# Attention scores over all 128 rows, and local keys in chunks of eight columns

## The chip, the cores and the metric

The kernel runs on one core of a Trainium2 chip. A core has five engines that run side by side: TensorE (PE, matrix products; its weight loads are listed apart as PEld), VectorE (DVE), ScalarE (ACT), GpSimd (POOL) and SyncE (SP), which here issues nearly all transfers; 16 DMA engines carry them. The metric is device time in microseconds, first to last work of one execution; lower is better.

## What is computed

The reference is one inference step of a two-layer backbone over 256 prompt tokens and 2048 latent tokens (a grid of 32 rows by 64 columns), in 1024 channels. Layer 0 is a convolution branch, layer 1 is attention with 16 heads of 64 channels. The part that the change touches is the attention of the latent tokens: each reads a window of 8 rows and 16 columns around it and all 512 cached context keys, in one softmax.

```
q = q * (HEAD_DIM ** -0.5)
# per row r of the grid; blocks j of 16 query columns, 32 key columns each
s_loc = einsum('bjqhd,brjkhd->bhjqrk', qb, k_blk)
s_loc = where(mask, s_loc + bias, NEG_INF)
s_ctx = einsum('bjqhd,blhd->bhjql', qb, k_ctx)
p = softmax(concatenate([s_loc, s_ctx]))
o = einsum(p_loc, v_blk) + einsum(p_ctx, v_ctx)
```

The bias depends on the distance of query and key in rows and columns. Everything is float32.

## The kernel before

**Precision.** Products run on numbers rounded to TensorE's shorter float32 form; each operand is kept as a rounded high part and the low rest, and products of high with high, high with low and low with high are added up. For the scores the keys of a head stand as 128 rows: 64 channels of one part, 64 of the other. `scores` multiplies them with the high part of the queries, held twice (rows 0 to 63 and 64 to 127), in a 128-row product (L1407), and then the half of the rows with the keys' high part with the low part of the queries, in a 64-row product (L1408).

**Stages.** Until about 1800 us of the span run the convolution layer and the projections of attention; there queries, keys and values are split and stored in scratch memory, and `masked_bias` subtracts the position bias from the window mask for every head (L1059). Then come the heads: two halves of eight heads, and in each half the prompt (two heads at a time) and four groups G of eight query rows. A group needs 11, 15, 15 or 12 rows of keys (`KEY_ROWS`).

**A unit** is one head, one group and one block j of 16 query columns: 128 queries against 512 context keys and 32 columns x R rows of local keys. There are 256 units for the latent tokens. A unit runs through these stages:
- four score products into a bank of accumulators S (`scores`, twice);
- on DVE a minimum over the context scores (L1474) and the sum with mask and bias with its minimum (L1476); scores are kept negated;
- on ACT the exponential with its sum (L1480), on DVE the reciprocal (L1481), on POOL the scaling (L1482);
- on TensorE eight transposes of the probabilities (L1492), on ACT their rounding (L1501), on DVE the rest (L109);
- for a pair of blocks the products with the values (L1517 for the context; L1520 or L1524 for the local keys).

**Order.** `attention` writes the order out by hand: a step of the pipeline issues the transposes of unit i - 2, the reductions of unit i, the values of a pair up to unit i - 3 or else a quarter of an output projection tile (`side_chunk`, L1625 to L1627), and then the scores of unit i + 1. TensorE and DVE keep that order; ACT, POOL and SP are ordered by a scheduler. S and the transposes' banks T are held twice. The loads of a head are issued a head ahead, into two buffers each of keys, bias and queries and three of values.

**Layouts.** Local keys, bias, mask, probabilities and values stand in the order (pair of columns, row, 2): the moving operand of the local products reads runs of two columns (8 bytes), each from another grid row. With pairs, ten columns share a product with the values where 10 R rows fit into 128 (groups 0 and 3, R = 11 and 12: `KEY_COLS` is 10); the others take eight (groups 1 and 2, R = 15). With ten, each block has its own four chunks of values, loaded in eight transfers; with eight, the chunks of a pair of blocks overlap, and five products serve both blocks.

Of the kernel before, what the change touches and what calls it, by code (L numbers as in the profile page):

```python
# [11 lines left out]
F32 = mybir.dt.float32  # L12
F32R = mybir.dt.float32r
# [5 lines left out]
P = 128  # L19
D = 1024  # L20
NK = D // P
NPR = 256
NSA = 2048
# [29 lines left out]
# times of the start: of a weight's load, rounding and rest; of the first products; of the modulation; of the input rows  # L53
# [11 lines left out]
# per group of eight query rows: first key row, number of key rows  # L65
KEY_ROWS = [(0, 11), (4, 15), (12, 15), (20, 12)]
# and the key columns that share a product with the probabilities: ten where their rows fit the array, else eight
KEY_COLS = [10, 8, 8, 10]
# per block of 16 query columns: first key column / 8, kind of column window, first bias column
# [6 lines left out]
class Kern:  # L76
    def __init__(self, ctx, tc, io):
# [13 lines left out]
        self.vs_d = d("vs_d", [GW // 2, NSA // GW, 2, NH, 2, DH])  # L91
# [9 lines left out]
    # ---------------------------------------------------------------- helpers  # L101
# [28 lines left out]
    # -------------------------------------------------------------- constants  # L130
    def constants(self):
# [7 lines left out]
        # vectors over channels, one column per 128 channels  # L139
# [7 lines left out]
    def vectors(self, name, srcs, change=None):  # L147
        """Vectors over channels are loaded; the function returned puts them as columns of 128 channels."""
# [23 lines left out]
    def more_constants(self):  # L172
        """The other vectors, in two steps."""
# [10 lines left out]
    def conv_constants(self):  # L184
        """Depthwise taps, [channel, tap], in two steps."""
# [99 lines left out]
    def modulated_steps(self, xts, layer, g, hi, lo, c0, name, rest, on_act=False, flush=(), wide=False):  # L285
        """Rows of xts (already scaled to unit rms), modulated, transposed and split, into columns c0.. of hi, lo."""
# [49 lines left out]
    def halves(self, src, shape, name):  # L336
        """A piece of a weight, rounded, and what is left of it."""
# [15 lines left out]
    # ------------------------------------------------------------- conv layer  # L353
    def conv_layer(self, part_a, part_b):
        """Input projection and depthwise convolution in two chunks of tokens; the second carries on where the first
        ends. Every operation is put at the time it is due by the tensor engine's rate, and all are issued in that
        order: the sums of the first taps of a channel tile run on Pool after its projection, those of the others on
        DVE after that. part_b are the blocks of the second chunk, made along the way."""
# [13 lines left out]
        for s in range(2 * NK):  # L372
# [93 lines left out]
            # the convolution, in two halves of the columns  # L466
# [48 lines left out]
            # the first half: Pool, then DVE in two sums; the second half: DVE, then Pool  # L515
# [28 lines left out]
        # the modulation and the input blocks of the first chunk  # L544
# [62 lines left out]
        # the norm of the first two tiles  # L607
# [13 lines left out]
        # the rest of the modulation, a part of it after each channel tile of the second chunk  # L621
# [5 lines left out]
        # the input blocks of the second chunk  # L627
# [74 lines left out]
        # variance by token on the partitions, then its root's inverse spread over all partitions  # L702
# [34 lines left out]
    def out_weight(self, w, name, res):  # L737
        """w, split, as four tiles of 16 KB per partition: [hi, lo][half of the rows]; two steps for 128 rows."""
# [12 lines left out]
    def conv_out(self, w, blocks, ready, res=None):  # L751
        """Output projection and residual; with res also the modulated input of the next layer."""
# [183 lines left out]
    def bias_rows(self, h):  # L936
        """Position bias of head h for every query of a tile, from row -4 and column -16 of the tile's first."""
# [4 lines left out]
    def na_values(self, blocks, then):  # L942
        """Values of some tokens, [token, channel]; then() where the weights that follow may be loaded."""
# [33 lines left out]
    def na_rest(self, blocks):  # L977
        """Keys, queries and gates of some tokens, [channel, token]."""
# [40 lines left out]
    def store_values(self, c, src, t0, pm):  # L1019
        """Values of four heads of 128 tokens as (hi, lo); those of the sample in the order (pair of columns, row, 2)."""  # L1020
# [21 lines left out]
    def masked_bias(self):  # L1042
        """Window mask less bias of every head, kind of row group and kind of column block: the scores are kept negated."""
# [5 lines left out]
        for h in range(NH):  # L1049
            raw = work([P, BIAS_LEN], "rows", 2, f"rb{h}")  # L1050
            nc.sync.dma_start(raw, self.bias_rows(h))
            for gk, G in enumerate((0, 1, 3)):
                r0, R = KEY_ROWS[G]
                b0 = r0 - 8 * G + 4
                view = lambda ap: ap[:, : 32 * R].rearrange("p (a r c) -> p a r c", a=16, c=2)
# [26 lines left out]
    def keys(self, ct, src, t0, n, pm, nm):  # L1082
        """Keys of two heads, stored as (hi, lo); those of odd heads as (lo, hi)."""
# [45 lines left out]
    def context_values(self):  # L1129
        """Cached values as (hi, lo)."""  # L1130
# [13 lines left out]
    def gated_weights(self):  # L1144
        """The weights of the last projection times the gate of either group, split."""
# [19 lines left out]
    # ------------------------------------------------------------------ phases  # L1165
# [569 lines left out]
```

## Time and profile before

| what | us |
|---|---|
| runs (three): lowest, median, highest | 3113.0, 3113.68, 3121.12 |
| profiled execution: span, first to last instruction | 3115.0 |
| heads of the latent tokens, 1840 to 3070 of the span | 1230 |

The page gives the profiled execution's time as its span alone; it lies 1.3 us above the median of the runs. In the timeline an instruction's row has its start, its duration, the engine, the line of the kernel, what it writes and reads, and the shape; "64*128" are the rows and columns of the weights on TensorE. Ends of products are modelled, so the time from one start to the next tells more than a duration. A row's bracket has the engine's idle time before it and what ended it.

### The profile page before, as it was taken

To read this page: it belongs to the slowest core of one execution; us is meant where nothing else is said; L and a number is where in the kernel's file an instruction comes from. 1 tells how busy PE (TensorE), PEld (TensorE's weight loads), DVE (VectorE), ACT (ScalarE), POOL (GpSimd) and SP (SyncE) were. 2 spreads that over 40 slices of the span, in tenths; PEclk is the share of its full clock that TensorE was granted. 3 is DMA by queue.
4 is the path that set the end of the run, shared out by engine and by line. 5 is a ranking of instruction groups with operands and counts; after the bars stand their busy time and mean duration, and the time that the engine had idled before them with its cause. 6 is when DMAs were issued, how large, how long until landed. Compare 5 with 4: busy or idle time off the path is not lost. (4 is left out here: it accounts for less than half of the span.)

```text
span 3115.0 us, 45374 instructions
## 1 busy us (share of the span) xinstructions
PE 3005.0 (96%) x15951; PEld 2328.0 (75%) x15951; DVE 1857.6 (60%) x3126; ACT 1427.7 (46%) x2538; POOL 1538.2 (49%) x1775
## 2 busy tenths in 40 slices
PE   6999999998999999999999989999999999999998
PEld 4888877775778989999888856666666666666666
DVE  4789999988865000345652046656566656666665
ACT  4466566775533222422222145555555545555553
POOL 4688877886533433622333133444444444444443
PEclk9999999998999999999999979999999999999999
DMA  6242554564355544689998445755545456555442
GB/s 232 86 136 90 197 188 156 183 198 161 122 169 159 149 127 131 187 242 315 347 328 265 125 149 183 204 144 144 143 136 172 137 176 204 164 145 142 132 136 99
DMA packets 429373, 537.40 MB, mean 173 GB/s; under 512 B 42066, under 2 KB 304042, under 8 KB 429017
## 3 DMA queue, kind: packets, MB, share of 16 engines
q1 hardware_dynamic: 429008, 530.42, 55.0%
q10 hardware_dynamic: 136, 4.07, 0.3%
q8 instruction: 127, 2.08, 0.3%
q14 instruction: 102, 0.83, 0.1%
HBM read 351.34 MB, written 187.13 MB: 173 GB/s over the span
## 5 line engine op out<-in xcount | busy, mean ns | idle before, releaser
L1482 POOL TENSOR_SCALAR sa_p<-sa_p,sa_m 128x992 f32<-128x992 f32 (+2 forms) x256 | 288.2, 1126 | 528.9 <-DVE sa_m L1481 424.9
L1501 ACT CAST sa_pt<-sa_T 128x512 fp32r<-128x512 f32 (+2 forms) x512 | 276.0, 589 | 540.9 <-PE sa_T L1492 540.8
L500 DVE SCALAR_TENSOR_TENSOR cv<-u,dw,cv 128x640 f32<-128x640 f32 (+2 forms) x570 | 427.9, 822 | 3.8 <-ACT cv L496 2.9
L1474 DVE TENSOR_REDUCE sa_m<-sa_S 128x1 f32<-128x512 f32 x256 | 176.9, 691 | 403.3 <-PE sa_S L1408 390.1
L109 DVE TENSOR_TENSOR sa_pt<-sa_T,sa_pt 128x512 fp32r<-128x512 f32 (+2 forms) x512 | 329.2, 684 | 4.1 <-ACT sa_pt L1501 3.8
L349 PE MATMUL ci_ps<-h_s_hi,ci_wh 128*128 128x512 f32 x768 | 307.1, 400 | 2.0 <-DVE shift L237 1.0
L1492 PEld LDWEIGHTS sa_T<-ident,sa_p 128*128 128x128 f32 (+2 forms) x2048 | 221.5, 140 | 115.0 <-issue 57.3
L351 PE MATMUL ci_ps<-h_s_hi,ci_wl 128*128 128x512 f32 x768 | 303.2, 395 | 0.0
L350 PE MATMUL ci_ps<-h_s_lo,ci_wh 128*128 128x512 f32 x768 | 302.9, 394 | 0.0
L1492 PE MATMUL sa_T<-ident,sa_p 128*128 128x128 f32 (+2 forms) x2048 | 284.1, 282 | 0.9 <-DVE sa_pt L109 0.9
L1480 ACT ACTIVATE sa_p<-sa_S,sa_m 128x992 f32<-128x992 f32 (+2 forms) x256 | 269.4, 1052 | 7.6 <-DVE sa_m L1476 4.5
L481 POOL TENSOR_TENSOR cv_s<-cv_s,cv_p 128x519 f32<-128x519 f32 (+1 forms) x155 | 233.3, 1505 | 69.7 <-DVE cv_s L504 49.0
L478 ACT ACTIVATE cv_p<-u,dw 128x640 f32<-128x640 f32 (+2 forms) x326 | 240.9, 770 | 55.0 <-POOL cv_s L481 35.7
L481 POOL TENSOR_TENSOR cv_p<-cv_p,cv_p 128x520 f32<-128x520 f32 (+1 forms) x155 | 227.7, 1469 | 26.8 <-ACT cv_p L478 19.2
L1407 PE MATMUL sa_S<-a_k,a_qh 128*128 128x480 f32 (+2 forms) x256 | 181.3, 708 | 0.0
L1408 PE MATMUL sa_S<-a_k,a_ql 64*128 64x480 f32 (+2 forms) x256 | 180.3, 704 | 0.0
L1517 PE MATMUL sa_O<-sa_pt,cv 128*128 128x256 f32 x1024 | 177.1, 295 | 0.3 <-DVE 3_14_of L1538 0.3
L1476 DVE CUSTOM_DVE_ANT_0 sa_S<-sa_S,a_bm,sa_m 128x480 f32<-128x480 f32 (+2 forms) x256 | 170.9, 668 | 9.0
L349 PEld LDWEIGHTS ci_ps<-h_s_hi,ci_wh 128*128 128x128 f32 x768 | 145.5, 189 | 39.2 <-ACT cv_p L478 2.5
L351 PEld LDWEIGHTS ci_ps<-h_s_hi,ci_wl 128*128 128x128 f32 x768 | 145.1, 189 | 33.6
L350 PEld LDWEIGHTS ci_ps<-h_s_lo,ci_wh 128*128 128x128 f32 x768 | 145.4, 189 | 31.1
L106 POOL TENSOR_TENSOR nis_wl<-nis_w,nis_wh 128x1024 fp32r<-128x1024 f32 x24 | 60.9, 2540 | 183.0 <-ACT nis_wh L341 157.8
(846 smaller groups left out, 7495.5 us busy)
## 6 DMA issues: line engine op xcount, KB each, us to landing
adaw<-in_ada_w SPq DMA_DIRECT2D x24, 1024.0 KB
ci_w<-in_conv_w_in SPq DMA_DIRECT2D x48, 512.0 KB
a_bm<-bm_d SPq DMA_DIRECT2D x32, 720.0 KB
x_s<-in_x_sample SPq DMA_DIRECT2D x32, 512.0 KB
vs_d<-v_s SPq DMA_DIRECT2D x128, 128.0 KB
a_qh<-qh_d SPq DMA_DIRECT2D x64, 256.0 KB
o_x<-x_d SPq DMA_DIRECT2D x32, 512.0 KB
a_v<-vs_d SPq DMA_DIRECT2D x128, 120.0 KB
```

The source lines that it names most:

```text
L109: self.nc.vector.tensor_tensor(out=lo, in0=src, in1=hi.bitcast(F32), op=ALU.subtract)
L349: self.nc.tensor.matmul(out, wh[:, k, :], hh[:, k, :], start=k == 0, stop=False)
L350: self.nc.tensor.matmul(out, wh[:, k, :], hl[:, k, :], start=False, stop=False)
L351: self.nc.tensor.matmul(out, wl[:, k, :], hh[:, k, :], start=False, stop=k == NK - 1)
L478: nc.scalar.activation(t, st["u"][:, c0 + tap : c1 + tap], AF.Copy, scale=self.dw[:, ct, tap : tap + 1])
L481: nc.gpsimd.tensor_tensor(out=st["sum", half], in0=st["sum", half], in1=st[half, tap], op=ALU.add)
L500: nc.vector.scalar_tensor_tensor(out=out, in0=u, scalar=w, in1=first, op0=ALU.mult, op1=ALU.add)
L1407: self.nc.tensor.matmul(out, q, k, start=True, stop=False)
L1480: nc.scalar.activation(p[:, n], S[:, n], AF.Exp, scale=-1.0, bias=m[:, 2:3], accum_out=m[:, 3:4])
L1482: nc.gpsimd.tensor_scalar(out=p[:, n], in0=p[:, n], scalar1=m[:, 3:4], scalar2=1.0, op0=ALU.mult, op1=ALU.mult)
L1492: nc.tensor.transpose(t[:w, c * P : c * P + P], p[:, x + c * w : x + c * w + w], self.ident)
L1501: nc.scalar.copy(pt[:w, 0, part, :, at], t)
```

## The change

It sets one chunk width, `CW = 8`, for all groups. Local keys, bias, mask, probabilities and values stand as (eight columns, row, 8); the low part of the queries is loaded for each head onto all 128 rows, as the high part is; both score products run over all 128 rows, so that low times low is added too; the value rows of a head come in one transfer. The separate treatment of groups 0 and 3 (ten columns, the block at the other end of its bank, the clearing of padding on POOL) is gone. Comments and docstrings are gone too, so line numbers shift by some 10 to 20 (`scores` from L1407 and L1408 to L1397 and L1398).

```
-KEY_COLS = [10, 8, 8, 10]
+CW = 8
-        self.vs_d = d("vs_d", [GW // 2, NSA // GW, 2, NH, 2, DH])
+        self.vs_d = d("vs_d", [GW // CW, NSA // GW, CW, NH, 2, DH])
...
-                view = lambda ap: ap[:, : 32 * R].rearrange("p (a r c) -> p a r c", a=16, c=2)
+                view = lambda ap: ap[:, : 32 * R].rearrange("p (a r c) -> p a r c", a=4, c=CW)
...
-        return bass.AP(ap.tensor, ap.offset, [ap.ap[0], [2, 16], [BIAS_COLS, R], [1, 2]])
+        return bass.AP(ap.tensor, ap.offset, [ap.ap[0], [CW, 4], [BIAS_COLS, R], [1, CW]])
...
-        hd.q = T("qh", [P, n], F32R, nm + "_qh")
-        src = self.qh_d[h * DH : h * DH + DH, a : a + n]
-        nc.sync.dma_start(hd.q.bitcast(F32), bass.AP(src.tensor, src.offset, [[0, 2], *src.ap]))
-        if b == 0:
-            hd.grp["ql"] = T("ql", [P, n], F32R, nm + "_ql")
-            nc.sync.dma_start(hd.grp["ql"].bitcast(F32), self.ql_d[rows, a : a + n])
-        else:
+        hd.q, hd.ql = (T(t, [P, n], F32R, f"{nm}_{t}") for t in ("qh", "ql"))
+        for t, d in ((hd.q, self.qh_d), (hd.ql, self.ql_d)):
+            src = d[h * DH : h * DH + DH, a : a + n]
+            nc.sync.dma_start(t.bitcast(F32), bass.AP(src.tensor, src.offset, [[0, 2], *src.ap]))
+        if b:
...
-        src = self.vs_d[:, r0 : r0 + R, :, hd.h].rearrange("a r c s d -> a (r c) (s d)")
-        if cw == 8:
-            for g in range(4):
-                self.nc.sync.dma_start(v[g * 2 * R : (g + 1) * 2 * R], src[g::4].rearrange("a x e -> x a e"))
-            return
-        for i, first in enumerate((0, 12)):
-            for c in range(4):
-                a = first + 5 * c
-                self.nc.sync.dma_start(v[: 10 * R, 4 * i + c], src[a : a + 5])
+        src = self.vs_d[:, r0 : r0 + R, :, hd.h].rearrange("a r c s d -> (r c) a (s d)")
+        self.nc.sync.dma_start(v[: CW * R], src)
...
-    def scores(self, out, q, ql, k, odd):
-        half = slice(DH, P) if odd else slice(0, DH)
+    def scores(self, out, q, ql, k):
         self.nc.tensor.matmul(out, q, k, start=True, stop=False)
-        self.nc.tensor.matmul(out, ql[half], k[half], start=False, stop=True)
+        self.nc.tensor.matmul(out, ql, k, start=False, stop=True)
...
-        kw = hd.k[:, :, 8 * JFIRST[j] : 8 * JFIRST[j] + 32].rearrange("p r (a c) -> p a r c", c=2)
+        kw = hd.k[:, :, CW * JFIRST[j] : CW * JFIRST[j] + 32].rearrange("p r (a c) -> p a r c", c=CW)
...
-        if wide:
-            x = 512 - 40 * R if jj else 512 + nl
-            nc.gpsimd.memset(p[:, x : x + 8 * R], 0.0)
-            at = 512 - 40 * R if jj else 512
...
-            for c in range(4) if cw == 10 else ():
-                nc.tensor.matmul(o, v[:w, 4 * pair + c].rearrange("p s d -> p (s d)"), loc[:, 256 * c : 256 * c + 256], start=False, stop=s == 1 and c == 3)
-            for c in (0, 4, 1, 2, 3) if cw == 8 else ():
+            for c in (0, 4, 1, 2, 3):
```

On TensorE the order of the steps is the same; what differs are the value products of groups 0 and 3. Here is the end of a step of group 0 before (values of head 0, then the scores of head 1, block 3; `cv` are context values, `a_0_v` the local ones, `ck` context keys, `a_1_k` local ones):

```order
L1517 MATMUL sa_0_O<-sa_0_2_pt,cv_16370 128x256 x4
L1520 MATMUL sa_0_O<-sa_0_2_pt,a_0_v 128x256 x4
L1407 MATMUL sa_1_3_S<-ck_16372,a_1_qh 128x512
L1408 MATMUL sa_1_3_S<-ck_16372,a_0_ql 128x512
L1407 MATMUL sa_1_3_S<-a_1_k,a_1_qh 128x352
L1408 MATMUL sa_1_3_S<-a_1_k,a_0_ql 128x352
```

And the same place on TensorE now:

```order
L1499 MATMUL sa_0_O<-sa_0_2_pt,cv_16372 128x256 x4
L1504 MATMUL sa_0_O<-sa_0_2_pt,a_0_v 128x128 x2
L1504 MATMUL sa_0_O<-sa_0_2_pt,a_0_v 128x256 x3
L1397 MATMUL sa_1_3_S<-ck_16374,a_1_qh 128x512
L1398 MATMUL sa_1_3_S<-ck_16374,a_1_ql 128x512
L1397 MATMUL sa_1_3_S<-a_1_k,a_1_qh 128x352
L1398 MATMUL sa_1_3_S<-a_1_k,a_1_ql 128x352
```

Four local value products of 256 columns have become two of 128 and three of 256, and head 1 reads low queries of its own (`a_1_ql`) instead of those shared with head 0.

On SP, the transfers of a head in group 0 (head 3, and the low queries of head 4) before, where `a_3_v` are value chunks and `a_3_bm` bias and mask:

```order
L1402 DMA a_3_v<-vs_d 110x1x128
L1367 DMA a_3_qh<-qh_d 128x1x512
L1359 DMA a_3_k<-ks_d 128x704
L1402 DMA a_3_v<-vs_d 110x1x128
L1364 DMA a_3_bm<-bm_d 128x3x352
L1402 DMA a_3_v<-vs_d 110x1x128 x6
L1370 DMA a_4_ql<-ql_d 128x512
```

And those of the same head on SP now:

```order
L1393 DMA a_3_v<-vs_d 88x8x128
L1370 DMA a_3_qh<-qh_d 128x1x512
L1361 DMA a_3_k<-ks_d 128x704
L1370 DMA a_3_ql<-ql_d 128x1x512
L1366 DMA a_3_bm<-bm_d 128x3x352
```

Eight transfers of values have become one that stands first, and the low queries of every head come before its bias.

More of the change, by code (lines that the diff above doesn't have):

```diff
@@ L1348, in load_head @@
                 nc.sync.dma_start(hd.q[:, e].bitcast(F32), bass.AP(src.tensor, src.offset, [[0, 2], *src.ap]))
-            hd.ql = T("ql", [P, n], F32R, nm + "_ql")
-            nc.sync.dma_start(hd.ql.bitcast(F32), self.ql_d[rows, a : a + n])
+            hd.ql = T("ql", [P, 2, NPR], F32R, nm + "_ql")
+            for e in range(2):
+                src = self.ql_d[(h + e) * DH : (h + e + 1) * DH, 0:NPR]
+                nc.sync.dma_start(hd.ql[:, e].bitcast(F32), bass.AP(src.tensor, src.offset, [[0, 2], *src.ap]))
             hd.v = T("vl", [P, 2, 4, DH], F32R, nm + "_v")
@@ L1364, in load_head @@
         nc.sync.dma_start(hd.bm[:, :, :nl], self.bm_d[h, GKIND[G]][:, :, :nl])
-        hd.q = T("qh", [P, n], F32R, nm + "_qh")
-        src = self.qh_d[h * DH : h * DH + DH, a : a + n]
-        nc.sync.dma_start(hd.q.bitcast(F32), bass.AP(src.tensor, src.offset, [[0, 2], *src.ap]))
-        if b == 0:
-            hd.grp["ql"] = T("ql", [P, n], F32R, nm + "_ql")
-            nc.sync.dma_start(hd.grp["ql"].bitcast(F32), self.ql_d[rows, a : a + n])
-        else:
+        hd.q, hd.ql = (T(t, [P, n], F32R, f"{nm}_{t}") for t in ("qh", "ql"))
[3 more added lines that the diff above has]
+        if b:
             hd.z = T("z", [P, n], F32, nm + "_z")
             nc.sync.dma_start(hd.z, self.zn_d[rows, a : a + n])
-        hd.ql = hd.grp["ql"]
         self.load_context(hd.ctx, h)
@@ L1418, in prompt_unit @@
                 cs = slice(u * P, u * P + P)
-                self.scores(S[:, (2 * e + u) * NPR : (2 * e + u + 1) * NPR], hd.q[:, e, cs], hd.ql[:, cs], hd.k[:, e], e)
+                self.scores(S[:, (2 * e + u) * NPR : (2 * e + u + 1) * NPR], hd.q[:, e, cs], hd.ql[:, e, cs], hd.k[:, e])
         yield
@@ L1463, in sample_unit @@
         S = self.bank("S", nm + "_S", 2, 1024)
-        cw = KEY_COLS[G]
-        wide, jj = cw == 10, j % 2
-        a, at = (512, 512 - nl) if wide and jj else (0, 512)
-        ctx, loc = S[:, a : a + 512], S[:, at : at + nl]
-        kw = hd.k[:, :, 8 * JFIRST[j] : 8 * JFIRST[j] + 32].rearrange("p r (a c) -> p a r c", c=2)
-        self.scores(ctx, hd.q[:, cs], hd.ql[:, cs], hd.ctx[h][0], b)
-        self.scores(loc, hd.q[:, cs], hd.ql[:, cs], kw, b)
+        jj = j % 2
+        ctx, loc = S[:, :512], S[:, 512 : 512 + nl]
+        kw = hd.k[:, :, CW * JFIRST[j] : CW * JFIRST[j] + 32].rearrange("p r (a c) -> p a r c", c=CW)
+        self.scores(ctx, hd.q[:, cs], hd.ql[:, cs], hd.ctx[h][0])
+        self.scores(loc, hd.q[:, cs], hd.ql[:, cs], kw)
         yield
@@ L1478, in sample_unit @@
         p = T("p", [P, 1024], F32, nm + "_p")
-        n = slice(min(a, at), min(a, at) + 512 + nl)
+        n = slice(0, 512 + nl)
         nc.scalar.activation(p[:, n], S[:, n], AF.Exp, scale=-1.0, bias=m[:, 2:3], accum_out=m[:, 3:4])
@@ L1482, in sample_unit @@
         nc.gpsimd.tensor_scalar(out=p[:, n], in0=p[:, n], scalar1=m[:, 3:4], scalar2=1.0, op0=ALU.mult, op1=ALU.mult)
-        if wide:
-            x = 512 - 40 * R if jj else 512 + nl
-            nc.gpsimd.memset(p[:, x : x + 8 * R], 0.0)
-            at = 512 - 40 * R if jj else 512
         yield
         ts = []
-        for part, w, x in ((0, P, a), (1, cw * R, at)):
+        for part, w, x in ((0, P, 0), (1, CW * R, 512)):
             t = self.bank("T", f"{nm}_T{part}", 2)
@@ L1498, in sample_unit @@
         for part, w, t in ts:
-            at = 1 - jj if part == 0 or wide else jj
+            at = 1 - jj if part == 0 else jj
             nc.scalar.copy(pt[:w, 0, part, :, at], t)
@@ L1511, in sample_values @@
         c0 = JFIRST[2 * pair]
-        cw = KEY_COLS[hd.G]
-        w = cw * KEY_ROWS[hd.G][1]
+        w = CW * KEY_ROWS[hd.G][1]
         for s in range(2):
@@ L1695, in neighbourhood_masks @@
             ok_c = (col >= cs[:, None]) & (col < cs[:, None] + KC)
-            ok = ok_c.reshape(P, 16, 1, 2) & ok_r.reshape(P, 1, R, 1)
+            ok = ok_c.reshape(P, 4, 1, CW) & ok_r.reshape(P, 1, R, 1)
             out[gk, :, jk, : 32 * R] = np.where(ok, 0.0, FAR).reshape(P, -1)
```

1 line of the change is left out of this document (removed).

## The prediction

> **What bounds the kernel now.** I read the page first for the shares, then the busy time of the attention stage by engine, then TensorE's timeline there row by row, because a busy TensorE says nothing of how fast each product goes.
>
> ```profile
> span 3115.0 us, 45374 instructions
> PE 3005.0 (96%) x15951; PEld 2328.0 (75%) x15951; DVE 1857.6 (60%) x3126; ACT 1427.7 (46%) x2538; POOL 1538.2 (49%) x1775
> 1840.00:3070.00 1230.00, 1208.91 (x6026) 805.34 (x6026) 760.70 (x1628) 638.93 (x1211) 545.51 (x881) 0.98 0.53 155
> ```
>
> The last row is the stage of the sample's heads (after the stretch: its length, busy time of PE, weight loads, DVE, ACT, POOL, then granted clock, DMA share, GB/s). TensorE is busy 1208.91 of 1230 us at a clock of 0.98; DVE 62%, ACT 52%, POOL 44%, the DMA engines 0.53. TensorE is the bound, and nobody else is near.
>
> Two steps of the pipeline on TensorE (start, duration, instruction; the next start is what counts, since durations overlap):
>
> ```profile
> 2109.43 1.09 PE L1492 MATMUL sa_T<-ident,sa_p 128*128 128x128 f32 x8
> ...
> 2110.59 0.39 PE L1626 MATMUL o<-w2l,0_1_y2h 128*128 128x512 f32 x1
> 2110.82 0.39 PE L1627 MATMUL o<-w2h,0_1_y2l 128*128 128x512 f32 x1
> ...
> 2111.75 0.40 PE L1407 MATMUL sa_S<-ck,a_qh 128*128 128x512 f32 x1
> 2112.08 0.49 PE L1408 MATMUL sa_S<-ck,a_ql 64*128 64x512 f32 x1
> 2112.50 0.77 PE L1407 MATMUL sa_S<-a_k,a_qh 128*128 128x480 f32 x1
> 2113.20 0.77 PE L1408 MATMUL sa_S<-a_k,a_ql 64*128 64x480 f32 x1
> 2113.90 1.09 PE L1492 MATMUL sa_T<-ident,sa_p 128*128 128x128 f32 x8
> ...
> 2116.36 0.74 PE L1524 MATMUL sa_O<-sa_pt,a_v 120*128 120x128 f32 x5
> 2116.94 0.39 PE L1407 MATMUL sa_S<-ck,a_qh 128*128 128x512 f32 x1
> ...
> 2119.07 1.09 PE L1492 MATMUL sa_T<-ident,sa_p 128*128 128x128 f32 x8
> ```
>
> A step with a piece of the output projection lasts 4.47 us (2109.43 to 2113.90), one with values 5.17 (to 2119.07), without a gap. A 128-row product of 512 contiguous columns is followed by the next start after 0.23 us (2110.59, 2110.82): 0.45 ns a column. The four score products of a unit take 0.33 + 0.42 + 0.70 + 0.70 = 2.15 us, where four products at 0.45 ns a column (512 + 512 + 480 + 480 columns) would take 0.89. That difference is what the change goes for, and it has two sources.
>
> ```profile
> L1408 PE MATMUL sa_S<-ck,a_ql 64*128 64x512 f32 x256 | 128.0, 500 | 0.4 <-DMA a_ql<-ql_d 0.4
> L1407 PE MATMUL sa_S<-ck,a_qh 128*128 128x512 f32 x256 | 103.7, 405 | 5.6 <-DMA a_qh<-qh_d 5.6
> L1407 PE MATMUL sa_S<-a_k,a_qh 128*128 128x480 f32 x128 | 98.4, 769 | 0.0
> L1408 PE MATMUL sa_S<-a_k,a_ql 64*128 64x480 f32 x128 | 97.8, 764 | 0.0
> L1407 PE MATMUL sa_S<-a_k,a_qh 128*128 128x384 f32 x64 | 42.4, 663 | 0.0
> ```
>
> *Rows.* The context products read contiguous keys, yet the pair takes 0.33 + 0.42 = 0.75 instead of 0.46: about 0.10 is lost going from 128 rows to 64 and 0.19 by the 64-row product that has 128 rows before and behind it. *Runs.* The local products with 128 and with 64 rows take the same (769 and 764 ns), so their length is no matter of rows; from 384 to 480 columns they grow by 106 ns, 1.1 ns a column, against 0.45 for contiguous keys. They read runs of two columns. Both local products have a change of rows ahead or behind: 0.70 less 0.19 leaves 0.51 for 480 columns, 1.06 ns each, the same figure from the other side.
>
> **The change part by part.** *All 128 rows in both score products.* The context pair falls from 0.75 to 0.46: 0.29 x 256 units = 74 us. (That loading 64 or 128 rows of weights might differ is excluded by rows that take 0.23 with 128.)
>
> *Runs of eight.* No row shows runs of eight; the ends are contiguous keys (0.45 ns a column) and runs of two (1.06). If each break between runs costs a fixed (1.06 - 0.45) x 2 = 1.2 ns, runs of eight cost 0.45 + 1.2 / 8 = 0.60. If instead a run takes the longer of 2.1 ns (what two columns take) and its own length, eight columns take 3.6 ns and the rate is 0.45. Both readings lie near the contiguous row; I take the middle, 0.52. The other two widths, before:
>
> ```profile
> 1911.53 0.62 PE L1407 MATMUL sa_S<-a_k,a_qh 128*128 128x352 f32 x1
> 1912.09 0.62 PE L1408 MATMUL sa_S<-a_k,a_ql 64*128 64x352 f32 x1
> 1912.64 1.09 PE L1492 MATMUL sa_T<-ident,sa_p 128*128 128x128 f32 x8
> ...
> 2410.44 0.67 PE L1407 MATMUL sa_S<-a_k,a_qh 128*128 128x384 f32 x1
> 2411.03 0.67 PE L1408 MATMUL sa_S<-a_k,a_ql 64*128 64x384 f32 x1
> 2411.63 1.09 PE L1492 MATMUL sa_T<-ident,sa_p 128*128 128x128 f32 x8
> ```
>
> Local pairs now: 1.40 us (480 columns, groups 1 and 2, 128 units), 1.19 (384, group 3, 64 units), 1.11 (352, group 0, 64 units). At 0.52: 0.50, 0.40, 0.37. Gain 0.90 x 128 + 0.79 x 64 + 0.74 x 64 = 213 us; at 0.45 it is 230, at 0.60 it is 193.
>
> The Trainium skill ("Advanced Engine Details and Errata", SBUF Cachelines) has 16-byte lines of which two consecutive hits suffice for full rate. Runs of two 4-byte columns hit a line twice, so by that rule they are not slow at all; 1.06 ns a column says otherwise, and the measurement decides. For runs of eight the rule gives the contiguous end, 230 us instead of 213 and a time lower by 17.
>
> *Values of groups 0 and 3.* Five products instead of four for each half (hi, lo) of a pair of blocks: 32 heads x 2 pairs x 2 halves = 128 times. Five take 0.58 (2116.36 to 2116.94, above), four take 0.48:
>
> ```profile
> 2409.20 0.64 PE L1520 MATMUL sa_O<-sa_pt,a_v 120*128 120x256 f32 x4
> 2409.68 0.40 PE L1407 MATMUL sa_S<-ck,a_qh 128*128 128x512 f32 x1
> ```
>
> 0.10 x 128 = 13 us lost, on the bound itself. The products and transposes then use 88 or 96 rows or columns, no width that the trace shows; the nearest rows, 110 and 120, flow like 128, so I take nothing. The other end is that they stall as 64 rows do: two halves x two changes x 0.19 x 64 pairs = 49 us.
>
> *Steps that TensorE did not bound by much.* What is late next is DVE's chain:
>
> ```profile
> 2109.60 0.69 DVE L1474 TENSOR_REDUCE sa_m<-sa_S 128x1 f32<-128x512 f32 x1 [2.21 <-PE sa_S L1408]
> ...
> 2112.42 0.16 DVE L1481 RECIPROCAL sa_m<-sa_m 128x1 f32<-128x1 f32 x1 [0.16 <-ACT sa_p L1480]
> 2112.61 0.69 DVE L1538 TENSOR_TENSOR 1_4_of<-sa_O,1_5_t 64x512 f32<-64x512 f32 x1
> ```
>
> 3.0 us a step from reduction to reciprocal, and 0.7 more in one step of a head's four: 12.7 a head. TensorE's new steps are 4.47 - 1.19 = 3.28 and 5.17 - 1.19 = 3.98, 14.5 a head, so it stays the bound there. Not in steps with neither values nor output work:
>
> ```profile
> 1867.52 1.10 PE L1492 MATMUL sa_T<-ident,sa_p 128*128 128x128 f32 x8
> ...
> 1870.32 0.88 PE L1492 MATMUL sa_T<-ident,sa_p 128*128 128x128 f32 x6
> ...
> 2959.70 1.09 PE L1492 MATMUL sa_T<-ident,sa_p 128*128 128x128 f32 x8
> ...
> 2962.55 0.66 PE L1492 MATMUL sa_T<-ident,sa_p 128*128 128x128 f32 x4
> ```
>
> These are the first and the last of 14 such steps, 2.8 to 3.1 us, already about DVE's 3.0: they keep their length, and 14 x 1.05 = 15 us of the gain is lost. 18 steps with half of a pair's values, counted in the same timeline, fall about 0.25 below DVE's chain: 5 more.
>
> *Loads.* The low halves of the queries come once a head, not once for two: 128 KB more a head on average, and values as one transfer instead of four or eight, of fewer bytes in groups 0 and 3. SyncE's issues of the eight cost 10.77 us for seven in one place, and near it lies the only long wait of TensorE in this stage:
>
> ```profile
> 1911.27 10.77 SPq L1402 DMA_DIRECT2D a_v<-vs_d  x7
> 1920.73 0.76 PE L1407 MATMUL sa_S<-ck,a_qh 128*128 128x512 f32 x1 [5.60 <-DMA a_qh<-qh_d]
> 2115.00:2117.00 2.00, 2.00 (x19) 2.00 (x18) 1.84 (x5) 1.86 (x4) 1.80 (x5) 1.00 1.02 287
> 2121.00:2123.00 2.00, 2.00 (x7) 0.84 (x5) 1.06 (x3) 1.03 (x2) 0.70 (x2) 1.00 0.12 47
> ```
>
> In groups 1 and 2 the engines run full for a while (1.02 at 287 GB/s) and then idle (0.12), so some 2.8 MB a head (keys 480 KB, bias 720, queries 512, values 480, gates 128, residual rows 512 by their tiles) fit into 14.5 us, but with less room than in 19.3. Bounds: 9 us won (that wait goes, with the slow step behind it) to 25 lost; I take 6 lost, for group 0, where the output weights arrive too.
>
> *Bias, masks, the stored order of the values.* Their work lies in the projections of attention. There DVE is busy 69 of 100 us under a TensorE that is busy 98:
>
> ```profile
> L1059 DVE TENSOR_TENSOR bm<-mask,rb 128x480 f32<-128x480 f32 x48 | 42.3, 934 | 3.3 <-DMA bm_d<-bm 3.3
> 1450.00:1550.00 100.00, 98.44 (x563) 86.76 (x562) 69.24 (x98) 24.62 (x42) 32.13 (x19) 1.00 0.99 341
> ```
>
> Same operations, longer runs: nothing, between a few microseconds either way if the transfers there, at 0.99, shift. POOL's dropped clearing of padding and the prompt's low halves: nothing, beside TensorE's work (the prompt's eight units could win 5).
>
> **Sum.** 74 + 213 - 13 - 20 - 6 = 248 off 3115.0 gives 2867; the median of the runs lies 1.3 below the profiled span, so **2866**.
>
> **Rivals.** *The gather stays slow:* a scattered read costs 1.06 ns a column whatever its runs. Then 74 + 0.19 x 2 x 256 = 171, less 13, 10 (fewer short steps hurt) and 6: 2972. For it: only contiguous and runs of two are in the trace. Against: 32-byte runs have a quarter of the breaks.
>
> *Rows do not matter*, and the 0.33 and 0.42 have another cause that stays: only the gather's gain, 2 x 0.54 ns x (480 x 128 + 384 x 64 + 352 x 64) = 117, less 13, 8 and 6: about 3024. The Trainium skill speaks for it ("TensorE: Matmul & The Clock Gate", "Why this matters for your kernels"): one product with few rows takes as long as one with 128. The rows speak against it: 500 against 405 ns for the same 512 columns, and 0.42 against 0.23 to the next start.
>
> *Narrow products stall* (88 and 96 rows): 49 us more, 2915. *Loads become a wait in most heads:* 64 heads x 1 us gives 2930.
>
> *Slower:* the single value transfer and the doubled low halves land so late that each head waits for its loads. A head takes 19.3 us now (twice 4.47 + 5.17); those 2.8 MB must come in that time, so the kernel gets slower only if the chip brings less than some 145 GB/s here; at 140, 64 heads x 0.7 us gives about 3160. Against it: 287 GB/s above.
>
> **How the numbers follow.** Forecast (2818 to 2910) 0.70; gather stays slow 0.10; rows do not matter 0.03; narrow products stall 0.05; loads wait 0.08; slower 0.03; nothing moves 0.01. The range goes down to 2818 (contiguous rate 17, loads 15 better, prompt 5, and 10 for the 0.01 us to which each of a unit's four starts is read) and up to 2915 (0.60 ns a column 20, loads 19 worse, or the stall of narrow products); it holds the forecast and about half of the two cases next to it. Within 0.3% (what a measurement can tell from no change) is 9 us: only if nothing moves or two rivals meet, 0.02; slower 0.03; faster 0.95.
>
> **What would show it.** Right: L1397 and L1398 on contiguous context keys both at about 405 ns with starts 0.23 apart; local ones of 480 columns with starts 0.22 to 0.29 apart; steps near 3.3 and 4.0 us; short steps unchanged at DVE's 3.0. Wrong: local starts still 0.5 apart, rows of TensorE waiting for a_qh, a_ql or a_v at heads' beginnings, or DVE's reciprocal ending after the next step's first transposes in most steps.

## The result, and the profile after

The changed kernel takes 3238.1 us (median of four runs, 3231.5 to 3242.8); the kernel before took 3114.7 beside it. The ratio is 1.040, 95% interval 1.038 to 1.041: **slower**, by 123 us, where I had forecast 248 us less.

First the page's head of the changed kernel, then the row of its heads by the windows view (columns as in the prediction: stretch, its length, busy time of PE, weight loads, DVE, ACT, POOL, then granted clock, DMA share, GB/s):

```profile
span 3239.6 us, 45214 instructions
...
PE 2801.7 (86%) x16079; PEld 2417.1 (75%) x16079; DVE 1858.0 (57%) x3126; ACT 1440.1 (44%) x2538; POOL 1501.6 (46%) x1647
```

```profile
1840.00:3160.00 1320.00, 999.04 (x6049) 881.84 (x6048) 756.20 (x1609) 645.53 (x1211) 508.49 (x747) 0.86 0.52 150
```

TensorE is busy 203 us less than before (2801.7 against 3005.0): the products did get cheaper. But among the heads it now works 999 of 1320 us instead of 1209 of 1230, at a clock of 0.86 instead of 0.98. No other engine is near its limit, and the DMA share is 0.52, as before. What TensorE waits for, by the view of waits from 1830 us on (what stood, in which line, for what; then total us, times, longest):

```profile
PE sa_S L1398 <- DMA a_ql<-ql_d: 213.8, 52, 7.9
PE sa_S L1397 <- DMA a_qh<-qh_d: 41.0, 16, 7.6
PE pa_S L1398 <- DMA aNone_ql<-ql_d: 34.7, 10, 5.5
...
PE pa_S L1397 <- DMA aNone_k<-ks_d: 8.8, 1, 8.8
...
PE pa_O L1442 <- DMA aNone_v<-vp_d: 5.6, 1, 5.6
```

That is 304 us for loads, 255 of it for the queries of the heads, in 68 places. One of them, on TensorE's timeline of the changed kernel, with a step of the forecast kind ahead of it (start, duration, instruction; in brackets the idle time before it):

```profile
2131.87 0.40 PE L1397 MATMUL sa_S<-ck,a_qh 128*128 128x512 f32 x1
2132.11 0.40 PE L1398 MATMUL sa_S<-ck,a_ql 128*128 128x512 f32 x1
2132.34 0.42 PE L1397 MATMUL sa_S<-a_k,a_qh 128*128 128x480 f32 x1
2132.59 0.42 PE L1398 MATMUL sa_S<-a_k,a_ql 128*128 128x480 f32 x1
2132.84 1.04 PE L1475 MATMUL sa_T<-ident,sa_p 128*128 128x128 f32 x8
...
2135.12 0.46 PE L1397 MATMUL sa_S<-ck,a_qh 128*128 128x512 f32 x1
2142.28 0.79 PE L1398 MATMUL sa_S<-ck,a_ql 128*128 128x512 f32 x1 [6.69 <-DMA a_ql<-ql_d]
...
2143.67 1.91 PE L1475 MATMUL sa_T<-ident,sa_p 128*128 128x128 f32 x8
```

The four score products of a unit start 0.24, 0.23, 0.25 and 0.25 us apart, 0.97 in all where they took 2.15. Then the next head's high part has come, its low part has not, and TensorE stands for 6.7 us. What the DMA engines do meanwhile, by windows of the changed kernel, and the DMA view of 2138 to 2141 us (packets, MB, share of the time of 16 engines):

```profile
2138.00:2140.00 2.00, 0.00 (x0) 0.00 (x0) 0.00 (x0) 0.00 (x0) 2.00 (x5) 0.76 0.13 49
2140.00:2142.00 2.00, 0.00 (x0) 0.00 (x0) 0.00 (x0) 0.00 (x0) 0.22 (x1) 0.50 0.14 52
```

```profile
DMA packets 72, 0.15 MB, mean 49 GB/s; under 512 B 0, under 2 KB 0, under 8 KB 72
...
q1 hardware_dynamic: 72, 0.15, 13.1%
```

This is the row to learn from. TensorE waits for a transfer while the DMA share is 0.13. A share of 13.1% of 16 engines is 2.1 engines: **two engines work without a pause and fourteen do nothing**. In the trace's records of the single transfers, exactly two are under way for 93% of these 3 us and three for the rest. They carry only packets of 2 KB (0.15 MB / 72), the size of a row of the queries' tiles, each in 0.131 x 16 x 3 us / 72 = 87 ns. A load of 256 KB is 128 such packets: over two engines 5.6 us. Before the change a head had one such load (the high part, with the two copies outermost in its source); its low part came as 128 plain rows and once for two heads. Now it has two. The row of 0.12 at 47 GB/s that the prediction quotes from the kernel before (2121 to 2123 us) is two engines' worth as well, and I read it as idleness. By the records its packets are of 5,760 bytes (rows of bias), 512 (values) and 4,096 (output rows), two at a time for most of it: what the two engines still had to carry of other loads, after all others were done.

The rest of the stage's traffic also passes through these two, by its sixteenth. Is that enough to fill them? The DMA view of the changed kernel, 1840 to 3160 us (issues: times, KB each):

```profile
q1 hardware_dynamic: 131865, 196.61, 51.9%
...
a_qh<-qh_d SPq DMA_DIRECT2D x63, 256.0 KB
a_ql<-ql_d SPq DMA_DIRECT2D x63, 256.0 KB
```

In engine-time 0.519 x 16 x 1320 = 10,960 us were worked. The queries' 126 loads are 126 x 128 x 87 ns = 1,400 of it, 700 on each of the two; of the other 9,560 each engine has 598. The two are busy for some 1,300 of 1,320 us, 98%, while the mean says 52%. This is an estimate; it takes all other traffic as spread evenly over the sixteen. The records of the single transfers agree with it: in these 1,320 us exactly two are under way for 36% of the time, some 480 us, and fewer than two for only 3%. In the heads of the kernel before it is 16% with two and 12% with fewer. That is the theory: **A, two DMA engines set the pace of the heads**. SyncE's issues fit a backlog too: one that takes 0.51 us elsewhere stood for 8 us, and the next load, that of the keys, could only be issued at 2140.89:

```profile
2125.75 0.51 SPq L1370 DMA_DIRECT2D a_ql<-ql_d  x1
...
2132.79 8.00 SPq L1370 DMA_DIRECT2D a_qh<-qh_d  x1
```

Against A stood **B**, the single transfer of values ahead of the queries delays them; **C**, the 128 KB more a head are too many bytes; and **D**, the low part stands behind other loads in SyncE's order.

### The profile page after: what moved, and what is told of

Its sections match the earlier page's. It is cut to its first block, busy times and chain, and to the rows that moved or that the text cites. A ratio compares the mean times of both kernels' runs of the same rounds, so it can differ in the third digit from the quotient of the medians.

```text
span 3239.6 us, 45214 instructions
## 1 busy us (share of the span) xinstructions
PE 2801.7 (86%) x16079; PEld 2417.1 (75%) x16079; DVE 1858.0 (57%) x3126; ACT 1440.1 (44%) x2538; POOL 1501.6 (46%) x1647
## 5 line engine op out<-in xcount | busy, mean ns | idle before, releaser
L1469 POOL TENSOR_SCALAR sa_p<-sa_p,sa_m 128x992 f32<-128x992 f32 (+2 forms) x256 | 280.2, 1095 | 744.7 <-DVE sa_m L1468 660.1
L1484 ACT CAST sa_pt<-sa_T 128x512 fp32r<-128x512 f32 (+3 forms) x512 | 278.3, 587 | 573.2 <-PE sa_T L1475 572.7
L109 DVE TENSOR_TENSOR sa_pt<-sa_T,sa_pt 128x512 fp32r<-128x512 f32 (+3 forms) x512 | 331.6, 683 | 7.6 <-ACT sa_pt L1484 3.1
L1475 PE MATMUL sa_T<-ident,sa_p 128*128 128x128 f32 (+3 forms) x2048 | 298.5, 294 | 14.1 <-DVE sa_pt L109 14.1
L1398 PE MATMUL sa_S<-ck,a_ql 128*128 128x512 f32 x256 | 118.0, 461 | 213.8 <-DMA a_ql<-ql_d 213.8
L1475 PEld LDWEIGHTS sa_T<-ident,sa_p 128*128 128x128 f32 (+3 forms) x2048 | 265.0, 148 | 46.1 <-POOL None_y1l L106 13.4
L1398 PEld LDWEIGHTS sa_S<-ck,a_ql 128*128 128x128 f32 x256 | 52.6, 206 | 237.6 <-DMA a_ql<-ql_d 235.0
L1504 PE MATMUL sa_O<-sa_pt,a_v 120*128 120x256 f32 (+5 forms) x1280 | 201.6, 290 | 1.3 <-DMA a_v<-vs_d 1.3
L1499 PE MATMUL sa_O<-sa_pt,cv 128*128 128x256 f32 x1024 | 192.5, 314 | 0.3 <-DVE 3_14_of L1518 0.3
L1504 PEld LDWEIGHTS sa_O<-sa_pt,a_v 120*128 120x128 f32 (+2 forms) x1280 | 179.7, 204 | 1.6 <-DMA a_v<-vs_d 1.6
```

Of the source, the lines that this page charges most:

```text
L109: self.nc.vector.tensor_tensor(out=lo, in0=src, in1=hi.bitcast(F32), op=ALU.subtract)
L1469: nc.gpsimd.tensor_scalar(out=p[:, n], in0=p[:, n], scalar1=m[:, 3:4], scalar2=1.0, op0=ALU.mult, op1=ALU.mult)
L1475: nc.tensor.transpose(t[:w, c * P : c * P + P], p[:, x + c * w : x + c * w + w], self.ident)
L1484: nc.scalar.copy(pt[:w, 0, part, :, at], t)
L1504: nc.tensor.matmul(dst, v[:w, c0 + c].rearrange("p s d -> p (s d)"), loc[:, lo:hi], start=False, stop=s == 1 and c == 3)
```

## The experiments

**The low halves in two loads of 64 rows.** Same bytes, one more issue; each load's outermost dimension is now 64 rows.

```
-        for t, d in ((hd.q, self.qh_d), (hd.ql, self.ql_d)):
-            src = d[h * DH : h * DH + DH, a : a + n]
-            nc.sync.dma_start(t.bitcast(F32), bass.AP(src.tensor, src.offset, [[0, 2], *src.ap]))
+        src = self.qh_d[h * DH : h * DH + DH, a : a + n]
+        nc.sync.dma_start(hd.q.bitcast(F32), bass.AP(src.tensor, src.offset, [[0, 2], *src.ap]))
+        for e in range(2):
+            nc.sync.dma_start(hd.ql[e * DH : e * DH + DH].bitcast(F32), self.ql_d[h * DH : h * DH + DH, a : a + n])
```

> The changed kernel, but the low halves of the queries come in two loads of 64 rows (one for each copy) instead of one load whose outermost dimension is the two copies. Same bytes, one more issue on SyncE per head. Theory A (a load with the two copies outermost is served by two DMA engines only: 128 packets of 2 KB at 84 ns each over two engines are 5.4 us, twice per head, in front of those engines' share of everything else): TensorE's waits for a_ql (213.8 us in the changed kernel's attention) fall below 30 us, the granted clock returns to 0.97 or more, and the time is 2850 to 2900 us. Theory B (the single value transfer delays what stands behind it): no change, 3238 within 20 us. Theory C (the 128 KB more per head are simply too many bytes): no change, 3238 within 20 us.

3031.6 us, 0.973 of before (0.971 to 0.976). Waits of this kernel from 1830 us on, and its heads by windows:

```profile
PE sa_S L1399 <- DMA a_ql<-ql_d: 60.9, 26, 5.5
PE sa_S L1398 <- DMA a_qh<-qh_d: 37.0, 9, 8.0
```

```profile
1840.00:2990.00 1150.00, 984.96 (x6226) 874.57 (x6227) 772.44 (x1655) 664.18 (x1245) 524.27 (x771) 0.92 0.65 176
```

207 us come back without a byte less, so B and C fall: C as a cause of these 207 us, B as the cause of the larger part. Yet it is 130 us short of what A expected, and the waits for a_ql are twice the 30 I allowed. My size was wrong: one load on two engines stays. By the rows above (an estimate, with 63 heads again) the two have 63 x 128 x 87 ns / 2 = 351 us of it and 704 of the rest, 1,055 of 1,150 us: 92%, still little room for loads that come in bursts; by the records exactly two transfers are under way for 21% of this time.

**Both halves in two loads of 64 rows** (the same edit for `qh`).

> As the run before, and the high halves in two loads of 64 rows too. Theory A: the two engines lose the second 5.4 us per head as well; the remaining waits for a_qh (41.0 us in the changed kernel) go down, and the time is 0 to 25 us below that of the run before, 2835 to 2890 us. No stretch in which the mean DMA share stands near 0.13 (two of sixteen) for longer than 2 us. Theories B and C: 3238 within 20 us.

2918.2 us, 0.938 (0.936 to 0.940). Waits of this kernel from 1830 us on:

```profile
PE pa_S L1399 <- DMA aNone_ql<-ql_d: 36.4, 10, 6.0
PE sa_T L1476 <- DVE sa_pt L109: 20.9, 12, 11.6
PE sa_S L1399 <- DMA a_ql<-ql_d: 10.9, 6, 3.3
```

The heads' queries are down from 255 to 11 us. What is left belongs mostly to the prompt, whose queries still have the two copies outermost. The time is 28 us above the range, and stretches with two engines alone, expected to be no longer than 2 us, are left: in 2328 to 2331 us, where the prompt's low halves are loaded, the share is again that of 2.2 engines, now with packets of 1 KB.

```profile
q1 hardware_dynamic: 137, 0.14, 13.5%
```

The gain over the run before is 113 us, not the 0 to 25 expected, for the reason just given.

**Controls.** Values in four loads again, low halves split by columns with the copies still outermost, and low halves issued by ScalarE:

```
+        for g in range(4):
+            self.nc.sync.dma_start(v[g * 2 * R : (g + 1) * 2 * R], src[g * 2 * R : (g + 1) * 2 * R])
```

> The changed kernel, but a head's values come in four loads of a quarter of the rows each (22 to 30 rows) instead of one. Theory A: no help, 3225 to 3270 us, TensorE's waits for a_ql stay above 180 us. Theory B (the single value transfer is the cause): the waits go, 2850 to 2900 us. Theory C: 3238 within 20 us.

```
+        for e in range(2):
+            src = self.ql_d[h * DH : h * DH + DH, a + e * n // 2 : a + (e + 1) * n // 2]
+            nc.sync.dma_start(hd.ql[:, e * n // 2 : (e + 1) * n // 2].bitcast(F32), bass.AP(src.tensor, src.offset, [[0, 2], *src.ap]))
```

> The changed kernel, but the low halves come in two loads that split the 512 columns and keep the two copies outermost in each. Same bytes, same number of loads as in the run that splits by rows, packets of 1 KB instead of 2. Theory A: each load still runs on two engines, 256 packets of 1 KB at 46 ns over two engines are 5.9 us: no help, 3230 to 3300 us. Rival (one load more, or a shorter load, is what helps): 2850 to 2900 us as with rows.

```
+            q = nc.sync if t is hd.q else nc.scalar
+            q.dma_start(t.bitcast(F32), bass.AP(src.tensor, src.offset, [[0, 2], *src.ap]))
```

> The changed kernel, but the low halves of the sample heads' queries are issued by ScalarE instead of SyncE, with the two copies still outermost. Theory A: the same two DMA engines serve both queues, so the change of queue does not help: 3200 to 3300 us. Rival D (the low halves are late because they stand behind other loads on SyncE, in its order of issue): TensorE's waits for a_ql fall under 60 us and the time under 3050 us.

They took 3289.2, 3255.0 and 3236.4 us, one run each. None helps. The first is 19 us above A's range; why four loads are worse than one was not pursued. Waits of TensorE, first with values in four loads (1840 to 3200 us), then with the low halves on ScalarE's queue (1840 to 3160 us):

```profile
PE sa_S L1399 <- DMA a_ql<-ql_d: 213.0, 51, 7.3
```

```profile
PE sa_S L1398 <- DMA a_qh<-qh_d: 190.4, 39, 12.3
```

The first removes B. In the second the wait has only changed its name: the low halves no longer stand in SyncE's line, so now the high halves come last, and the time is the same. D falls; another queue did not bring more engines. The DMA view of this run, 1974 to 1977 us, has packets of both queues side by side (q1 is SyncE's, q10 has the low halves), and together they still fill no more than 2.1 engines:

```profile
q1 hardware_dynamic: 37, 0.07, 6.6%
q10 hardware_dynamic: 36, 0.07, 6.4%
```

The split by columns tells that it isn't the number of loads that helped: two loads by rows brought 207 us, two by columns lost 17.

**The prompt too.** All loads of queries on 64 rows.

> As the run with both halves of the sample heads' queries in two loads of 64 rows (2918 us), and the prompt heads' queries in such loads too (they still had the two copies outermost, packets of 1 KB on two engines). Theory A: the waits that were left, 36.4 us of pa_S for aNone_ql, 9.3 for aNone_k and the single 11.6 us for which DVE stood behind aNone_z, go, and the time falls by 40 to 60 us to 2855 to 2880 us, my forecast for the whole change. Rival (the prompt's waits are latency of loads that are issued too late, not bandwidth of two engines): 2905 to 2925 us.

2865.6 us (2859.2 to 2867.2), 0.919 of before (0.916 to 0.921): the fastest of all, and 373 us below the changed kernel with the same products and the same bytes, so C falls altogether. Its page's head, and its waits over the whole span:

```profile
span 2865.3 us, 45461 instructions
...
PE 2710.9 (95%) x16079; PEld 2343.5 (82%) x16079; DVE 1846.7 (64%) x3126; ACT 1443.8 (50%) x2538; POOL 1505.2 (53%) x1647
```

```profile
PE sa_T L1478 <- DVE sa_pt L109: 24.3, 15, 13.8
PE sa_S L1401 <- DMA a_ql<-ql_d: 12.1, 4, 3.4
...
PE pa_S L1401 <- DMA aNone_ql<-ql_d: 9.1, 8, 2.2
```

The account of the 374 us between the two spans closes: 304 less 21 us of waits for these loads from 1830 us on (12.1 for a_ql, 3.2 for a_qh, 5.5 for the prompt's low halves), and 2801.7 less 2710.9 = 91 us of work by the same 16079 products. That work is a matter of the clock: by the traces' clock records TensorE worked 265 us of the whole span at a granted clock of 0.50 in the changed kernel and 79 us in this one, and half of the difference is 93. The 13.8 us for DVE (it stands behind the load of the prompt's gates) had been expected to go and did not.

**What of the gain belongs to what.** Three more kernels, all with their queries loaded by 64 rows: the kernel before with nothing else changed; the fastest kernel with its low product back on 64 rows and the low halves shared by two heads again, which leaves the runs of eight (and the single transfer of values) alone; and the kernel before with 128 rows, which leaves the rows alone. The main lines of their edits, in this order:

```
+        for e in range(2):
+            nc.sync.dma_start(hd.q[e * DH : e * DH + DH].bitcast(F32), src)
```

> The kernel before the change, with nothing but the high halves of the queries in two loads of 64 rows (sample and prompt heads). Theory A: there the two engines were loaded once per head, not twice, and TensorE hardly waited for them (5.6 us once): 3095 to 3114 us, within 0.6 per cent of before. Rival (the two-engine loads cost the kernel before as well, spread over everything): 3070 us or less.

```
+        half = slice(DH, P) if odd else slice(0, DH)
         self.nc.tensor.matmul(out, q, k, start=True, stop=False)
-        self.nc.tensor.matmul(out, ql, k, start=False, stop=True)
+        self.nc.tensor.matmul(out, ql[half], k[half], start=False, stop=True)
```

> The changed kernel with all query loads on 64 rows, but the low product back on the 64 rows of one head with the low halves shared by two heads: only the runs of eight are left of the change (with the five value products of groups 0 and 3). By the rows of the kernel before: 0.54 ns x 2 x (480 x 128 + 384 x 64 + 352 x 64) = 117 us won, 13 + 8 lost: about 96 below the kernel before with the same loads, 2995 to 3030 us. Rival (the rows do not matter): as low as the run with everything, 2855 to 2880 us.

```
-            hd.grp["ql"] = T("ql", [P, n], F32R, nm + "_ql")
-            nc.sync.dma_start(hd.grp["ql"].bitcast(F32), self.ql_d[rows, a : a + n])
+        hd.ql = T("ql", [P, n], F32R, nm + "_ql")
+        src = self.ql_d[h * DH : h * DH + DH, a : a + n]
+        for e in range(2):
+            nc.sync.dma_start(hd.ql[e * DH : e * DH + DH].bitcast(F32), src)
...
-        self.nc.tensor.matmul(out, ql[half], k[half], start=False, stop=True)
+        self.nc.tensor.matmul(out, ql, k, start=False, stop=True)
```

> The kernel before with its pairs of columns, but both score products over 128 rows, all query loads on 64 rows: only the rows are left of the change. By the rows of the kernel before: 74 us on the context pair and 0.19 x 2 x 256 = 97 on the local pair, less some 10 in short steps: 2935 to 2975 us. Rival (the rows do not matter): 3095 to 3114 us. Rival (the local pair, read in pairs of columns, is bound by its reads whatever the rows): 74 us alone, 3025 to 3045 us.

| all queries loaded by 64 rows | median us | ratio to before | 95% interval |
|---|---|---|---|
| before (pairs of columns, 64 rows) | 3085.2 | 0.990 | 0.987 to 0.992 |
| runs of eight alone | 3007.8 | 0.965 | 0.962 to 0.967 |
| rows alone | 2935.2 | 0.942 | 0.940 to 0.944 |
| both | 2865.6 | 0.919 | 0.916 to 0.921 |

The two-engine loads cost the kernel before as well, 30 us, more than I allowed in A and less than the rival's 45. The 14 us that TensorE waited for loads in its attention are gone, and the same products take 13 us less (2991.9 against 3005.0). Of the change itself the runs bring 77, the rows 150, both 220; the first two times lie where their expectations put them, and both rivals there (rows without effect; a pair bound by its reads whatever the rows) fall. The score products one by one, first with the runs alone, then with the rows alone, then with both, by the timelines of these kernels:

```profile
2013.52 0.51 PE L1400 MATMUL sa_S<-a_k,a_qh 128*128 128x480 f32 x1
2013.96 0.52 PE L1401 MATMUL sa_S<-a_k,a_ql 64*128 64x480 f32 x1
```

```profile
2010.79 0.69 PE L1411 MATMUL sa_S<-a_k,a_qh 128*128 128x480 f32 x1
2011.28 0.72 PE L1412 MATMUL sa_S<-a_k,a_ql 128*128 128x480 f32 x1
```

```profile
2100.39 0.40 PE L1400 MATMUL sa_S<-a_k,a_qh 128*128 128x480 f32 x1
2100.62 0.42 PE L1401 MATMUL sa_S<-a_k,a_ql 128*128 128x480 f32 x1
```

From the high product to the low one it is 0.70 us before, 0.44 with the runs, 0.49 with the rows and 0.23 with both. The two costs add: 0.21 for the change of rows and 0.26 for the pairs of columns at 480 columns, taken away in either order.

**Rows alone, loads on two engines.** If two engines set the pace, then TensorE's own work should hardly matter.

```
-        for e in range(2):
-            nc.sync.dma_start(hd.ql[e * DH : e * DH + DH].bitcast(F32), src)
+        nc.sync.dma_start(hd.ql.bitcast(F32), bass.AP(src.tensor, src.offset, [[0, 2], *src.ap]))
```

(and the same for `qh` and for the prompt)

> As the run with the rows alone (pairs of columns, both products over 128 rows, 2935 us), but both halves of the queries again in loads with the two copies outermost, as in the changed kernel. Theory A: the pace of a head is set by two DMA engines that serve 256 packets of 2 KB for the queries (11 us) and their sixteenth of all else (10 us by the changed kernel's mean share), so the time no longer depends on what TensorE needs: 3190 to 3290 us, near the changed kernel's 3238 although TensorE has 70 us more work. Rival (the loss needs the runs of eight or the single value transfer): 2930 to 3000 us.

3327.7 us, 1.069 of before (1.067 to 1.071), and 392 us above the same products with loads by 64 rows. Waits of this kernel from 1840 us on:

```profile
PE sa_S L1408 <- DMA a_ql<-ql_d: 205.8, 50, 7.9
PE sa_S L1407 <- DMA a_qh<-qh_d: 54.2, 20, 9.5
```

So the loss needs neither the runs of eight nor the single transfer of values. But it is 38 us above the range and 90 above the changed kernel, not the same pace. This kernel still has the older value transfers, four or eight a head; whether they put more on the two engines was not tried and stays open.

## Why the prediction was wrong

*The step that failed is the one on loads.* "I take 6 lost", with bounds of 9 won and 25 lost, came out as 343 lost: at equal loads the change won 220 us, as it stands it lost 123. (The changed kernel is 373 us above its twin with loads by 64 rows, 3238.1 less 2865.6; 30 of a cost of this kind the kernel before had already.) I priced bytes: "some 2.8 MB a head" at the stage's rate. The trace had a sign of the true price: I quoted a share of 0.12 at 47 GB/s and called it idle. Twelve hundredths are two of sixteen, and the question to ask was why two engines still have work when the others have none. Then 128 packets of 2 KB on two engines give 5.6 us, and a second such load a head leaves no room.

The Trainium skill ("DMA: Bandwidth & Descriptors", "Why a DMA increments its semaphore by 16 and not by 1") has the rule that I left out: the number of engines is the largest count up to 16 that divides the slowest dimension of both sides, and its "Rules for kernel authors" warn of a leading broadcast of a few copies. For a source whose slowest dimension is the two copies that gives two engines; the trace agrees with its 2.1.

*The rival on the other side was the right one, with the wrong condition.* It named the place (the doubled low halves land late, each head waits), and let it happen "only if the chip brings less than some 145 GB/s". The changed kernel moved 150 GB/s in the mean of its heads and waited all the same, because a mean over sixteen engines says nothing of two. Its other half, the single transfer of values, is cleared by the controls. The milder rival, a wait in most heads of 1 us, had the place right too; the heads' waits were 255 us in 68 places, 3.7 each, and dearer by the clock that falls in them.

*Context pair, 74 us:* right. 2293.04, 2293.27 and 2293.49 below are 0.45 for the pair; the forecast was 0.46.

```profile
2291.40 0.74 PE L1507 MATMUL sa_O<-sa_pt,a_v 96*128 96x128 f32 x5
2291.98 0.63 PE L1502 MATMUL sa_O<-sa_pt,cv 128*128 128x256 f32 x4
...
2293.04 0.39 PE L1400 MATMUL sa_S<-ck,a_qh 128*128 128x512 f32 x1
2293.27 0.39 PE L1401 MATMUL sa_S<-ck,a_ql 128*128 128x512 f32 x1
2293.49 0.36 PE L1400 MATMUL sa_S<-a_k,a_qh 128*128 128x384 f32 x1
```

(TensorE's timeline of the fastest kernel, in group 3.)

*Local products, 213 us:* right, by the starts. 480 columns take 0.23 to 0.25 us to the next start where 0.52 ns a column gave 0.25; runs of eight flow nearly like contiguous keys, and the split of the old 0.70 into 0.19 for the rows and 0.51 for the pairs was right as well (0.21 and 0.49 measured). The two ends of this term were added up a little wide: by their own rates they are 229 and 196, not 230 and 193; nothing hangs on it.

*Narrow products:* no stall. In the rows above five products of 96 rows take 0.58 us, as five of 120 rows did before, and five of 88 rows in group 0 of the same kernel the same 0.58 (1843.96 to 1844.54); so the 0.10 a time for five instead of four stands as well. *Short steps, 20 lost:* not measured apart.

*The sum at equal loads* was 254 without the term for loads and came out at 220. Where the other 34 went the windows tell. First the kernel before with its queries by 64 rows, then the fastest kernel at the same stretch, and ten microseconds of it:

```profile
1840.00:2040.00 200.00, 198.99 (x1022) 132.48 (x1022) 133.31 (x297) 109.23 (x204) 86.37 (x148) 1.00 0.66 196
```

```profile
1840.00:2040.00 200.00, 166.99 (x1089) 148.86 (x1089) 138.02 (x308) 115.79 (x212) 84.61 (x128) 0.92 0.82 208
1850.00:1860.00 10.00, 0.00 (x0) 0.00 (x0) 0.00 (x0) 0.00 (x0) 0.00 (x0) 0.72 1.06 211
2040.00:2240.00 200.00, 197.74 (x1324) 175.88 (x1323) 161.90 (x349) 139.00 (x249) 107.01 (x153) 1.00 0.74 201
```

At the start of the heads (group 0, with context keys, values and output weights arriving) all sixteen engines run full, and a faster TensorE loses 32 us of 200 there; afterwards it is busy 198 of 200 again. Of these 32 us, 14 are one wait: VectorE stands for the load of the prompt's gates, and TensorE behind it.

```profile
1860.79 0.43 DVE L1530 TENSOR_TENSOR aNone_z<-None_of,aNone_z 128x256 f32<-128x256 f32 x1 [13.75 <-DMA aNone_z<-zn_d]
```

So my "6 lost, for group 0" was too small even where the loads are well spread. This is read from the windows and the timeline and was not tested by a run. Nor do such windows add up to 34 exactly: from 2240 to 2440 us TensorE is busy 184 of 200, and a part of losses like these was priced already in the 20 for short steps. That the fastest kernel's 2865.6 us equals my 2866 is therefore partly chance: 30 us come from a kind of load that the kernel before had already, and about as much is missing from the sum.

## What to carry to other kernels

Before adding a load, read how many engines loads of its kind keep busy: in a stretch where only such a load is under way, that is the DMA share times 16. A load whose outermost dimension is two copies, as here, is worth cutting into one load a copy, with the rows outermost; in this case that alone was worth 373 us, and 30 in the kernel that seemed to have no trouble with its transfers. When a change makes the bounding engine faster, ask of each transfer whether it fits the new pace on the engines that carry it, not whether the bytes fit the mean.

## What the runs showed of the hardware

- Loads with two copies outermost ran on 2.1 of 16 DMA engines (72 packets of 2 KB in 3 us, 87 ns each). Two such loads from two queues, SyncE's and ScalarE's, shared 2.1 engines as well (73 packets in 3 us), and the time did not change (3236.4 us).
- A change between 128 and 64 rows costs a product about 0.2 us even when its moving operand is read slowly: 0.21 us at 480 columns in pairs or in eights. The two costs do not hide each other.
- A stall of 6.7 us cost more than itself: the granted clock stood at 0.50 from 2140 us to nearly 2146, and the eight transposes behind it took 1.91 us where they take 1.04.
